# Low parts of 68 weight tiles of a decoder layer: written by ScalarE and an accumulating DMA in place of a subtraction on GpSimd

## The chip, the cores and the metric

The kernel runs on one core of a Trainium2 chip. The metric is the device time of one execution in microseconds (us). Below, PE is TensorE, DVE VectorE, ACT ScalarE, POOL GpSimd and SP SyncE, as the profile names them.

## The reference

One layer with three sub-layers, each ending in a LayerNorm over a residual sum. `u` is the modulated input of 512 rows and 1024 columns.

```python
# 1 and 3: SwiGLU feed-forward, 1024 -> 2 x 2816 -> 1024
# 2: token mixing
u = x * (1.0 + sc2) + sh2
q, k, v, glu_a, glu_b, gate_a, gate_b = jnp.split(u @ w_in[l], split_idx, axis=-1)   # 7 x 1024 columns
y_sb = stick_breaking_attention(heads(q), heads(k), heads(v))      # 16 heads of 64, strictly causal
y_sb = y_sb.transpose(0, 2, 1, 3).reshape(bsz, seq, SB_WIDTH) @ w_sb_out[l]
y_conv = conformer_conv(glu_a, glu_b, conv_w[l], conv_b[l], conv_ln_g[l], conv_ln_b[l]) @ w_conv_out[l]
merged = jax.nn.sigmoid(gate_a) * y_sb + jax.nn.sigmoid(gate_b) * y_conv
x = layer_norm(DEEPNORM_ALPHA * x + g2 * (merged @ w_out[l]), ln2_g[l], ln2_b[l])
```

`conformer_conv` is a causal convolution over 31 positions of each channel, then a LayerNorm and a swish. All data are float32.

## The kernel before

Every matrix product is made of three products in a shorter format (F32R): a value is split into a high part (a cast) and a low part (the value less its high part), and high x high, high x low and low x high are summed in PSUM. A weight tile of 128 x 1024 (512 KB) is loaded into one of three `raw` buffers, then `split_w` makes two tiles of it, `whi` by a cast on ACT (L113) and `wlo` by a subtraction, `raw - whi`, on POOL or DVE (L114). There are five buffers of each. `load_w` does this with POOL; `load_gated`, for weights that are scaled by a gate first (L127, on POOL), does it with DVE.

The second sub-layer, from about 405 to 1010 us, is written as a list of tasks. Each tile task has a part that fetches and splits a weight tile and one or two parts that multiply: `tile_tasks` for a block of 128 columns of q, k, the two halves of the GLU, or the gates ga and gb (24 PE instructions a tile), `v_tasks` for two tiles of w_v and four row blocks (psv, L594 to L596), `proj_tasks` for the output projections ysb and ycv. The first four tiles of w_in (q, k and the GLU halves of block 0) go through `dense_group` and are not touched by the change.

- Attention runs in 64 units (8 pairs of heads, 2 heads, 4 blocks of 128 rows). Unit i: three products give scores z; ACT makes two sigmoids of them (nb and be, L623, L624); DVE scans nb (L625); POOL masks be (L628) and multiplies it by nb (L630). Two units later PE transposes be into pw (L640), ACT casts it to wTh (L643), DVE makes the low part wTl (L644), and one unit after that PE multiplies with v into po (L663 to L665). Between the units stand the tile tasks, whose weights are fetched three tasks ahead.
- The convolution is made on DVE: for each of 8 channel blocks 31 taps (L511, L513 and 29 or so fused multiply-adds at L515) into cacc, and a sum (L520). They stand in a background list, from which 3.8 are taken for each attention unit and 14 after each ysb tile.
- When all taps are done, the convolution's rows are transposed on PE (pt, L766), normalised on DVE (cn, L776), transposed back (ptb, L787) and passed through a swish on ACT (L790). Then come the ycv projections. Meanwhile DVE also makes modulation vectors of the next sub-layer (ada, L179), whose rows are loaded into a ring of two buffers.

The order on each engine is set by a scheduler when the program is built; each engine then works through its own list in that order and waits for semaphores of the others. SP issues the loads (L101) in the same way.

Of the kernel before, what the change touches and what calls it, by code (L numbers as in the profile page):

```python
# [7 lines left out]
F32 = mybir.dt.float32  # L8
F32R = mybir.dt.float32r
BF16 = mybir.dt.bfloat16  # L10
AF = mybir.ActivationFunctionType
ALU = mybir.AluOpType
PSUM = bass.MemoryType.PSUM

P = 128
# [28 lines left out]
def decoder_block(ctx: ExitStack, tc: tile.TileContext, a: dict, out: bass.AP):  # L44
    nc = tc.nc

    core = ctx.enter_context(tc.tile_pool(name="core", bufs=1))
    wts = ctx.enter_context(tc.tile_pool(name="wts", bufs=1))
# [16 lines left out]
    def bank(name, tag="ps"):  # L65
        return banks["pool"].tile([P, 512], F32, tag=tag, name=name, bufs=banks["bufs"][tag])
# [33 lines left out]
    def load(dst, src, chain=False):  # L100
        ins = nc.sync.dma_start(dst, src).ins  # L101
        if "last" in issued:
            tc.add_manual_dep(ins, issued["last"].name,
                              mybir.DependencyInfo(mybir.DependencyClass.NoSync, mybir.DependencyReason.DATA),
                              reason="first loads in order of use")
        if chain:
            issued["last"] = ins


    def split_w(raw, lo_eng):  # L110
        hi = wts.tile([P, 1024], F32R, align_bytes=256, tag="whi", name="whi", bufs=5)
        lo = wts.tile([P, 1024], F32R, align_bytes=256, tag="wlo", name="wlo", bufs=5)
        nc.scalar.copy(hi, raw)  # L113
        lo_eng.tensor_sub(lo, raw, hi.bitcast(F32))  # L114
        return hi, lo

    def raw_tile(src, chain=False):
        raw = wts.tile([P, 1024], F32, tag="raw", name="raw", bufs=3)
        load(raw, src, chain)
        return raw  # L120

    def load_w(src, lo_eng=None):
        return split_w(raw_tile(src), lo_eng or nc.gpsimd)

    def load_gated(src, G):
        raw = raw_tile(src)
        nc.gpsimd.tensor_mul(raw, raw, G)  # L127
        return split_w(raw, nc.vector)

    def dense(ps, w, u, c0=0, c1=S, k0=0, k1=KC):  # L130
        (wh, wl), (uh, ul) = w, u
        for k in range(k0, k1):
            ks = slice(k * P, (k + 1) * P)
            nc.tensor.matmul(ps[:, c0:c1], wh[:, ks], mov(uh, k)[:, c0:c1], start=(k == 0), stop=False)  # L134
            nc.tensor.matmul(ps[:, c0:c1], wh[:, ks], mov(ul, k)[:, c0:c1], start=False, stop=False)  # L135
            nc.tensor.matmul(ps[:, c0:c1], wl[:, ks], mov(uh, k)[:, c0:c1], start=False, stop=(k == KC - 1))  # L136
# [229 lines left out]
    def dense_group(names, srcs, u, first, tags=None):  # L366
        ws = [load_w(s, nc.vector if first and i in FIRST_DVE else None) for i, s in enumerate(srcs)]
        pss = [bank(n, tag) for n, tag in zip(names, tags or ["ps"] * len(names))]
        if first:
            for c in range(2):  # L370
                for i, (ps, w) in enumerate(zip(pss, ws)):
                    dense(ps, w, u, c * 256, c * 256 + 256)
                    if c == 0 and i in LATE_AT and late:
                        late.pop(0)()
        else:
            for ps, w in zip(pss, ws):
                dense(ps, w, u)
        return pss
# [153 lines left out]
    def half_dense(st, name, ks, done):  # L532
        if ks == 0:
            st["ps"] = bank(name)
        dense(st["ps"], st["w"], u2, 0, S, ks * 4, ks * 4 + 4)
        if ks == 1:
            done(st["ps"])


    def tile_tasks(src, name, done):  # L540
        st = {}
        return [(lambda: st.update(w=load_w(src)), lambda: half_dense(st, name, 0, done)),
                (None, lambda: half_dense(st, name, 1, done))]

    def set_qk(j, x, ps):
# [2 lines left out]
    def qk_tasks(j):  # L548
        out_ = []
        for x, col in (("q", 0), ("k", 8)):  # L550
            out_ += tile_tasks(a["w_in"][col + j], x, lambda ps, x=x: set_qk(j, x, ps))
        return out_
# [11 lines left out]
    def glu_tasks(j):  # L564
        st = {}
        return (tile_tasks(a["w_in"][24 + j], "glua", lambda ps: st.update(a=ps))
                + tile_tasks(a["w_in"][32 + j], "glub", lambda ps: glu_done(j, st["a"], ps)))
# [10 lines left out]
    def v_tasks(q):  # L578
        st = {}

        def block(t):
            if t == 0:
                st["h"] = ap_.tile([P, NT, 256], F32R, tag="vh", name="vh", bufs=2)
                st["l"] = ap_.tile([P, NT, 256], F32R, tag="vl", name="vl", bufs=2)
                vq[q] = (st["h"], st["l"])
            if t % 2 == 0:
                st["ps"] = bank("psv")
            ps = st["ps"]
            o = ps[:, (t % 2) * 256 : (t % 2) * 256 + 256]
            tsl = slice(t * P, (t + 1) * P)  # L590
            for k in range(KC):
                wh, wl = st["w"][k // 4]
                cs = slice((k % 4) * 256, (k % 4) * 256 + 256)
                nc.tensor.matmul(o, u2[0][:, k, tsl], wh[:, cs], start=(k == 0), stop=False)  # L594
                nc.tensor.matmul(o, u2[0][:, k, tsl], wl[:, cs], start=False, stop=False)  # L595
                nc.tensor.matmul(o, u2[1][:, k, tsl], wh[:, cs], start=False, stop=(k == KC - 1))  # L596
            if t % 2 == 1:
                dst = st["h"][:, t - 1 : t + 1, :]
                pv = ps.rearrange("p (t e) -> p t e", t=2)
                nc.scalar.copy(dst, pv)  # L600
                nc.vector.tensor_sub(st["l"][:, t - 1 : t + 1, :], pv, dst.bitcast(F32))

        def fetch():
            st["w"] = [load_w(a["w_v"][q, h]) for h in range(2)]

        return [(fetch if t == 0 else None, lambda t=t: block(t)) for t in range(NT)]

# [101 lines left out]
    done = fetched = 0  # L709
# [93 lines left out]
    def proj_tasks(name, w, u, j, done):  # L803
        st = {}

        def half(ks):
            if ks == 0:
                st["ps"] = bank(name)
            dense(st["ps"], st["w"], u, 0, S, ks * 4, ks * 4 + 4)
            if ks == 1:  # L810
                done(j, st["ps"])

        return [(lambda: st.update(w=load_w(w[j])), lambda: half(0)), (None, lambda: half(1))]

    def sb(j):
        return proj_tasks("ysb", a["w_sb"], yp2, j, sb_done)
# [40 lines left out]
    for j in range(KC):  # L857
        if j + 2 < KC:
            run(gate_tasks("gb", j + 2))
        prefetch(2)  # L860
        run(proj_tasks("ycv", a["w_cv"], cp2, j, merge_done))
        bg(2)
# [115 lines left out]
```

## Time and profile before

| What | Value |
|---|---|
| Time, median of 3 runs | 1391.4 us (1390.05 to 1391.75) |
| The profiled execution | 1388.65 us, its span 1387.0 us |
| Busy, share of the span | PE 94%, DVE 59%, POOL 49%, ACT 33% |
| POOL's subtractions (L114) | 156, 398.7 us, 2560 ns each |
| ACT's casts of weights (L113) | 212, 220.8 us, 1046 ns each |
| DMA | 162.22 MB, mean 117 GB/s |

The span is the time from the first to the last instruction in the trace; the time of the execution has a little more around it. An engine's busy share is an average over the three sub-layers, which are limited by different things. In rows of waits, "PE po L664 <- DVE wTl L644: 19.4, 20, 4.6" reads: PE's instructions at L664 that write po waited for DVE's at L644 that write wTl, 19.4 us in total, 20 times, 4.6 us at the longest.

### The profile page before, as it was taken

How to read it: one execution, taken by the hardware profiler on the slowest of the kernel's cores; microseconds unless marked ns; L12 is line 12 of the kernel's file. 1: busy time of each engine (PE TensorE's matmuls, PEld its weight loads, DVE VectorE, ACT ScalarE, POOL GpSimd, SP SyncE). 2: the span in 40 equal slices, each digit the busy share in tenths (PEclk: the TensorE clock that was granted, in tenths of full speed). 3: DMA queues.
4: the chain of work that ended last, by engine and by line, in shares of the span. 5: the costliest groups of instructions: out<-in, count | busy, mean ns of one | idle time of the engine just before them, and what ended most of it. 6: DMA issues, size and time to landing. Idle time of an engine off the chain costs nothing.

```text
span 1387.0 us, 16644 instructions
## 1 busy us (share of the span) xinstructions
PE 1303.7 (94%) x6444; PEld 1076.4 (78%) x6444; DVE 817.2 (59%) x1017; ACT 458.0 (33%) x725; POOL 683.2 (49%) x392
## 2 busy tenths in 40 slices
PE   6899999999999998989998994998999999999997
PEld 4688888888897777767776873786898888888886
DVE  7876910454546968699899998516485100014545
ACT  2332322222254343434442422522263222222230
POOL 3474544644136675845555542355145366555433
PEclk9999999999999999999999997999999999999999
DMA  9669832323122221321122425323155233332221
GB/s 356 209 225 324 284 109 92 106 91 107 61 92 77 61 77 31 91 61 47 62 61 61 137 106 170 120 90 107 61 200 165 91 98 115 106 106 92 92 76 61
DMA packets 48063, 162.22 MB, mean 117 GB/s; under 512 B 5600, under 2 KB 5744, under 8 KB 47984
## 3 DMA queue, kind: packets, MB, share of 16 engines
q1 hardware_dynamic: 47952, 161.15, 35.6%
q8 instruction: 50, 0.82, 0.2%
q14 instruction: 29, 0.24, 0.1%
q0 software_dynamic: 32, 0.01, 0.0%
HBM read 159.04 MB, written 2.10 MB: 116 GB/s over the span
## 4 chain that ended last, share of the span: by engine, by line
PE 69%; DVE 25%; DMA 2%; issue 2%; POOL 1%; ACT 1%; SPq 0%; DVEq 0%; POOLq 0%; ACTq 0%
PE y L345 19%; DVE cacc L515 13%; DVE ada L179 3%; DVE nb L625 2%; DVE wTl L644 1%; PE psv L594 1%; PE gb L136 1%; PE gb L135 1%; PE ycv L135 1%; PE ycv L136 1%; PE gb L134 1%; PE ycv L134 1%; PE psv L596 1%; PE psv L595 1%; DMA ada<-in_ada_t 1%
## 5 line engine op out<-in xcount | busy, mean ns | idle before, releaser
L114 POOL TENSOR_TENSOR wlo<-raw,whi 128x1024 fp32r<-128x1024 f32 x156 | 398.7, 2560 | 363.2 <-ACT whi L113 351.3
L113 ACT CAST whi<-raw 128x1024 fp32r<-128x1024 f32 x212 | 220.8, 1046 | 407.5 <-issue 75.3
L515 DVE SCALAR_TENSOR_TENSOR cacc<-h,cv_w,cacc 128x512 f32<-128x512 f32 x232 | 237.0, 1080 | 0.0
L127 POOL TENSOR_TENSOR raw<-raw,mod_g 128x1024 f32<-128x1024 f32 x52 | 130.3, 2511 | 140.2 <-DMA raw<-in_dn 71.5
L114 DVE TENSOR_TENSOR wlo<-raw,whi 128x1024 fp32r<-128x1024 f32 x56 | 111.5, 1991 | 24.8 <-ACT whi L113 24.8
L345 PE MATMUL y<-whi,sh 128*128 128x512 f32 x352 | 113.8, 390 | 0.0
L345 PE MATMUL y<-wlo,sh 128*128 128x512 f32 x352 | 113.6, 389 | 0.0
L345 PE MATMUL y<-whi,sl 128*128 128x512 f32 x352 | 113.5, 389 | 0.0
L630 POOL TENSOR_TENSOR be<-be,nb 128x127 f32<-128x127 f32 (+1 forms) x64 | 53.4, 834 | 105.2 <-DVE nb L625 94.0
L179 DVE SCALAR_TENSOR_TENSOR ada<-ada,crow 128x512 f32<-128x512 f32 x96 | 91.8, 996 | 18.7 <-DMA ada<-in_ada_t 13.0
L410 DVE TENSOR_TENSOR sl<-sF,sh 128x512 fp32r<-128x512 f32 x44 | 45.3, 1031 | 85.1 <-ACT sh L409 85.1
L345 PEld LDWEIGHTS y<-wlo,sh 128*128 128x128 f32 x352 | 66.1, 188 | 13.7
L345 PEld LDWEIGHTS y<-whi,sl 128*128 128x128 f32 x352 | 66.1, 188 | 13.7
L345 PEld LDWEIGHTS y<-whi,sh 128*128 128x128 f32 x352 | 66.1, 188 | 13.6
L409 ACT CAST sh<-sF 128x512 fp32r<-128x512 f32 x44 | 27.1, 623 | 143.8 <-PE y L345 132.0
L625 DVE TENSOR_TENSOR_SCAN nb<-nb,future 128x127 f32<-128x127 f32 (+1 forms) x64 | 63.4, 990 | 1.4 <-ACT nb L623 1.4
L643 ACT CAST wTh<-pw 128x128 fp32r<-128x128 f32 (+1 forms) x64 | 27.2, 425 | 79.7 <-PE pw L640 79.6
L664 PE MATMUL po<-wTl,vh 128*64 128x128 f32 x160 | 32.9, 231 | 19.4 <-DVE wTl L644 19.4
L212 DVE SCALAR_TENSOR_TENSOR acc<-ada,silu_c,acc 128x1024 f32<-128x1024 f32 x21 | 43.7, 2080 | 12.3 <-DMA ada<-in_ada_w 11.9
L628 POOL TENSOR_SCALAR_AFFINE_SELECT be<-be 128x128 f32<-128x128 f32 x64 | 41.1, 642 | 8.9 <-ACT be L624 8.9
L452 PE MATMUL first<-uh,whi 128*128 128x512 f32 x64 | 27.2, 426 | 18.7 <-DVE uh L448 11.5
L664 PEld LDWEIGHTS po<-wTl,vh 128*64 128x64 f32 x160 | 21.7, 136 | 28.7 <-DVE wTl L644 25.3
(490 smaller groups left out, 3297.4 us busy)
## 6 DMA issues: line engine op xcount, KB each, us to landing
raw<-in_gu SPq DMA_DIRECT2D x80, 512.0 KB, 3.6
raw<-in_w_in SPq DMA_DIRECT2D x48, 512.0 KB, 3.6
raw<-in_dn SPq DMA_DIRECT2D x44, 512.0 KB, 3.5
ada<-in_ada_t SPq DMA_DIRECT2D x32, 512.0 KB, 4.5
ada<-in_ada_w SPq DMA_DIRECT2D x24, 512.0 KB, 4.7
ada<-in_ada SPq DMA_DIRECT2D x32, 256.0 KB, 6.0
raw<-in_gu_first SPq DMA_DIRECT2D x8, 512.0 KB, 6.5
raw<-in_w_v SPq DMA_DIRECT2D x8, 512.0 KB, 3.4
```

The costliest lines, as they stand in the source:

```text
L113: nc.scalar.copy(hi, raw)
L114: lo_eng.tensor_sub(lo, raw, hi.bitcast(F32))
L127: nc.gpsimd.tensor_mul(raw, raw, G)
L179: nc.vector.scalar_tensor_tensor(raw[:, qs], raw[:, qs], 1.0, crow[:, qs], ALU.mult, ALU.mult, accum_out=parts[:, q : q + 1])
L212: nc.vector.scalar_tensor_tensor(acc, raw, sc[:, k : k + 1], acc, ALU.mult, ALU.add)
L345: nc.tensor.matmul(acc[t][h][:, c0 - h * 512 : c1 - h * 512], st[:, tsl], wt[:, c0:c1], start=(k == 0 and i == 0 and c0 % 512 == 0), stop= ...
L410: nc.vector.tensor_sub(sl, sF[f], sh.bitcast(F32))
L515: ins = nc.vector.scalar_tensor_tensor(o, hv, cv_w[:, j, i : i + 1], o, ALU.mult, ALU.add)
L625: nc.vector.tensor_tensor_scan(nb[:, 1:n][:, ::-1], nb[:, 1:n][:, ::-1], future[:, S - n + 1 : S][:, ::-1], 1.0, ALU.mult, ALU.max)
L628: nc.gpsimd.affine_select(be[:, n - P : n], be[:, n - P : n], [[-1, P]], ALU.is_gt, 0.0, base=0, channel_multiplier=1)
L630: nc.gpsimd.tensor_mul(be[:, 0 : n - 1], be[:, 0 : n - 1], nb[:, 1:n])
L664: nc.tensor.matmul(po[0:DH, tsl], vh[:, sb, vs], wl[:, ss], start=False, stop=False)
```

## The change

A new function, `load_added`, takes the place of `load_w` in `tile_tasks`, `v_tasks` and `proj_tasks`: 44 tiles of w_in, 8 of w_v, 8 of w_sb and 8 of w_cv, 68 in all. ACT writes the cast `whi` as before, then the negative of it into `wlo`; POOL issues a DMA that reads the weight tile from HBM once more and adds it to `wlo` in place. The subtractions for the feed-forward sub-layers, the first four tiles of w_in and the gated weights stay.

```diff
+    def load_added(src):
+        raw = raw_tile(src)
+        hi = wts.tile([P, 1024], F32R, align_bytes=256, tag="whi", name="whi", bufs=5)
+        lo = wts.tile([P, 1024], F32R, align_bytes=256, tag="wlo", name="wlo", bufs=5)
+        nc.scalar.copy(hi, raw)
+        nc.scalar.mul(lo, hi.bitcast(F32), -1.0)
+        nc.gpsimd.dma_start(out=lo, in_=src, accum_op=ALU.add)
+        return hi, lo
...
-        return [(lambda: st.update(w=load_w(src)), lambda: half_dense(st, name, 0, done)),
+        return [(lambda: st.update(w=load_added(src)), lambda: half_dense(st, name, 0, done)),
...
-            st["w"] = [load_w(a["w_v"][q, h]) for h in range(2)]
+            st["w"] = [load_added(a["w_v"][q, h]) for h in range(2)]
...
-        return [(lambda: st.update(w=load_w(w[j])), lambda: half(0)), (None, lambda: half(1))]
+        return [(lambda: st.update(w=load_added(w[j])), lambda: half(0)), (None, lambda: half(1))]
```

In the changed program the cast is L130, the negative L131 and the DMA L132, and later lines stand ten further down. The lists of PE and DVE hold the same instructions in the same order as before. On POOL, early in attention, where the mask (AFFINE_SELECT) and the product of be stand between the weights' low parts, the list before is:

```order
L628 AFFINE_SELECT be_3255<-be_3255 128x128
L630 TENSOR_TENSOR be_3255<-be_3255,nb_3254 128x383
L114 TENSOR_TENSOR wlo_3560<-raw_3557,whi_3559 128x1024
L628 AFFINE_SELECT be_3292<-be_3292 128x128
L628 AFFINE_SELECT be_3336<-be_3336 128x128
L630 TENSOR_TENSOR be_3292<-be_3292,nb_3291 128x511
L304 TENSOR_TENSOR n0_2596<-n0_2596,raw_3327 128x1024
L114 TENSOR_TENSOR wlo_3673<-raw_3670,whi_3672 128x1024
```

and of the change, at the same place:

```order
L638 AFFINE_SELECT be_3260<-be_3260 128x128
L640 TENSOR_TENSOR be_3260<-be_3260,nb_3259 128x383
L638 AFFINE_SELECT be_3297<-be_3297 128x128
L132 DMA wlo_3567<-in_w_in 128x1024
L638 AFFINE_SELECT be_3341<-be_3341 128x128
L640 TENSOR_TENSOR be_3297<-be_3297,nb_3296 128x511
L314 TENSOR_TENSOR n0_2596<-n0_2596,raw_3332 128x1024
L640 TENSOR_TENSOR be_3341<-be_3341,nb_3340 128x127
L132 DMA wlo_3681<-in_w_in 128x1024
```

Each subtraction has become an issue of a DMA at about the same place in the list, one or two steps later.

On ACT, in the same units, where the casts of weights stand between attention's casts (wTh) and sigmoids (nb, be), the list before is:

```order
L113 CAST whi_3559<-raw_3557 128x1024
L525 CAST qh_3273<-q_3233 128x512
L643 CAST wTh_3279<-pw_3277 128x128
L623 ACTIVATE nb_3291<-z_3287 128x512
L624 ACTIVATE be_3292<-z_3287 128x512
L643 CAST wTh_3319<-pw_3316 128x256
L623 ACTIVATE nb_3335<-z_3331 128x128
L624 ACTIVATE be_3336<-z_3331 128x128
L113 CAST whi_3672<-raw_3670 128x1024
L525 CAST kh_3366<-k_3298 128x512
L643 CAST wTh_3380<-pw_3376 128x384
```

and of the change:

```order
L130 CAST whi_3566<-raw_3564 128x1024
L535 CAST qh_3278<-q_3238 128x512
L653 CAST wTh_3284<-pw_3282 128x128
L633 ACTIVATE nb_3296<-z_3292 128x512
L634 ACTIVATE be_3297<-z_3292 128x512
L131 ACTIVATE wlo_3567<-whi_3566 128x1024
L653 CAST wTh_3324<-pw_3321 128x256
L633 ACTIVATE nb_3340<-z_3336 128x128
L634 ACTIVATE be_3341<-z_3336 128x128
L130 CAST whi_3680<-raw_3678 128x1024
L535 CAST kh_3373<-k_3303 128x512
L131 ACTIVATE wlo_3681<-whi_3680 128x1024
```

The negative (L131) stands a few steps behind its cast, ahead of a later unit's wTh; nothing else changes places.

## The prediction, made before the changed kernel had run

> **What bounds the kernel now.** I read the page's chain first, then the busy time of the second sub-layer by stages, then what TensorE (PE) waits for there. The page's span and its chain, by engine and by line:
>
> ```profile
> span 1387.0 us, 16644 instructions
> PE 69%; DVE 25%; DMA 2%; issue 2%; POOL 1%; ACT 1%; SPq 0%; DVEq 0%; POOLq 0%; ACTq 0%
> ```
>
> PE carries the end, but a quarter of the chain lies on VectorE (DVE). The stages of the second sub-layer, one row each: attention with the convolution taps, the first output projections, the convolution's normalisation, the second projections. Columns: window, its length, busy us of PE, weight loads, DVE, ACT and POOL, granted clock, DMA share, GB/s.
>
> ```profile
> 428.00:757.00 329.00, 303.81 (x1799) 242.27 (x1798) 287.99 (x344) 131.00 (x271) 205.82 (x180) 0.98 0.20 62
> 757.00:828.00 71.00, 71.00 (x324) 58.82 (x323) 68.65 (x82) 23.45 (x30) 30.41 (x12) 1.00 0.35 117
> 828.00:876.00 48.00, 24.67 (x123) 19.75 (x122) 42.26 (x86) 16.68 (x37) 13.57 (x9) 0.79 0.50 167
> 876.00:962.00 86.00, 85.63 (x378) 70.59 (x376) 30.11 (x40) 26.43 (x36) 41.02 (x17) 1.00 0.34 104
> ```
>
> PE is idle 25.2 us in the first row (329.00 - 303.81) and 23.3 us in the third; in the second and fourth it is full. DVE is 88% busy in the first (287.99 of 329), 97% in the second and 88% in the third. PE's waits from 428 to 880 us (sum, times, longest):
>
> ```profile
> PE po L664 <- DVE wTl L644: 19.4, 20, 4.6
> PE ptb L787 <- DVE cn L776: 13.6, 3, 11.4
> PE pt L766 <- DVE cacc L520: 9.7, 1, 9.7
> PE k L134 <- DVE ql L526: 4.0, 2, 3.6
> PE psv L594 <- DVE vl L601: 1.6, 1, 1.6
> ```
>
> All five end on DVE: 48.3 us, as much as the two idle sums (48.5). POOL, whose work is removed, ends none of them. So the question is whether POOL's subtraction costs DVE anything. One subtraction on POOL, and the convolution tap that DVE runs at that moment, alone and with its two followers:
>
> ```profile
> 780.72 2.68 POOL L114 TENSOR_TENSOR wlo<-raw,whi 128x1024 fp32r<-128x1024 f32 x1 [2.78 <-ACT whi L113]
> 781.06 2.88 DVE L515 SCALAR_TENSOR_TENSOR cacc<-h,cv_w,cacc 128x512 f32<-128x512 f32 x1
> 781.06 4.21 DVE L515 SCALAR_TENSOR_TENSOR cacc<-h,cv_w,cacc 128x512 f32<-128x512 f32 x3
> ```
>
> The tap that meets the subtraction takes 2.88 us and ends with it; two more taps add 1.33 us, 0.665 us each. DVE stands still while POOL subtracts. All taps (nanoseconds min/median/max) and their busy time in the two stretches; the subtractions of both, and those in the first alone (nothing on DVE, 92.91 us on POOL):
>
> ```profile
> L515 DVE SCALAR_TENSOR_TENSOR cacc<-h,cv_w,cacc x232: 721/743/2907, 431.8 to 837.1; 128x512 f32<-128x512 f32 x116
> 428.00:757.00 329.00, 172.60 (x173) 0.98 0.20 62
> 757.00:876.00 119.00, 64.42 (x60) 0.91 0.41 137
> L114 POOL TENSOR_TENSOR wlo<-raw,whi x52: 2338/2479/4408, 426.3 to 872.9; 128x1024 fp32r<-128x1024 f32 x52
> 428.00:757.00 329.00, 0.00 (x0) 92.91 (x37) 0.98 0.20 62
> ```
>
> At 0.665 us each, 173 taps would take 115.0 us and 60 would take 39.9: the taps lose 57.6 and 24.5 us, 82.1 in all, to waiting for POOL.
>
> **The change, part by part.** It takes 68 subtractions off POOL (44 tiles of w_in, 8 of w_v, 8 of w_sb and 8 of w_cv; 52 of them in the row above) and adds, for each, an ACT pass over 128x1024, an issue on POOL and an accumulating DMA of 512 KB. TensorE's and DVE's orders stay as they are. The nearest rows of the additions: ACT's cast and its multiplication of a tile of that shape, the only DMA that POOL issues now (time on POOL, then time to landing), and the plain load of the same weights.
>
> ```profile
> L113 ACT CAST whi<-raw 128x1024 fp32r<-128x1024 f32 x212 | 220.8, 1046 | 407.5 <-issue 75.3
> L298 ACT ACTIVATE raw<-raw x4: 1059/1060/1061, 416.6 to 1153.5; 128x1024 f32<-128x1024 f32 x4
> L420 POOL DMA_DIRECT2D vec<-in_vecs x1: 735/735/735, 1.9 to 1.9; - x1
> vec<-in_vecs POOLq DMA_DIRECT2D x1, 8.0 KB, 5.7
> raw<-in_w_in SPq DMA_DIRECT2D x48, 512.0 KB, 3.6
> ```
>
> *POOL* goes from 52 x 2.48 = 129 us to 52 x 0.735 = 38 us in that stretch, and its attention steps (be) queue behind 0.7 instead of 2.5 us.
>
> *When the weights are ready.* Now a low part takes 2.48 us behind ACT's cast; afterwards 1.06 (ACT) + 0.74 (issue) + the landing. No row shows an accumulating DMA: the landing lies between 3.6 us (a load of that size) and 5.7 + 3.6 = 9.3 us (POOL's small DMA, plus a second pass over the bytes). I take 6: 7.8 us instead of 2.5. What hides it is the ring of five buffers:
>
> ```profile
> ACT whi L113 <- PE gb L135: 22.0, 5, 4.4
> L134 PE MATMUL gb<-uh,whi x64: 389/389/478, 874.3 to 944.5; 128*128 128x512 f32 x64
> L136 PE MATMUL ycv<-ph,wlo x64: 388/389/389, 891.2 to 961.2; 128*128 128x512 f32 x64
> ```
>
> ACT's cast waits for PE to leave the fifth-last tile, and 16 tiles (8 gb, 8 ycv) take 874.3 to 961.2 us, 5.43 each: a lead of four tiles, 21.7 us, even where PE is full. So the later arrival costs nothing there at 7.8 us, nor at the upper end's 11.1; without that cover it would be 5 to 9 us per tile. One place has less cover, the second weight tile of the first v block:
>
> ```profile
> 406.35 1.05 ACT L113 CAST whi<-raw 128x1024 fp32r<-128x1024 f32 x1 [6.43 <-PE q L135]
> L595 PE MATMUL psv<-wlo,uh x32: 283/283/283, 415.0 to 426.1; 128*128 128x256 f32 x32
> ```
>
> Its cast ends at 407.4; qh's cast (a fraction of a us) stands between it and the new pass, so the low part lands near 416 us; block t=0 needs it about 1.4 us after 415.0 (the four blocks take 11.1 us, 2.8 each, and the second tile serves the second half). That costs 0 to 3 us once; I take 1.
>
> Beside these rows the Trainium skill has a rule that speaks against the change: "Collectives: The Full Stack", section "The bandwidth ceiling: the fold count and why AG ≠ RS ≠ AR", says that an add in the DMA path reads two sources for each chunk written and so runs at half of a copy's rate. By it the landing would be an estimated 2 x 3.6 = 7.2 us, the weights 9.0 us behind the cast, and the sum below unchanged; no run here shows it yet.
>
> *SP.* The raw tile is free once ACT has cast it, no longer when POOL has subtracted, so loads go out about 2.5 us earlier; SP's order shifts at one place only (a load of crow and two of ada). Nothing waits for that: 0. *DMA.* 68 x 0.524 = 36 MB more are read in the sub-layer; the DMAs' share is 0.20 to 0.50 of the engines in the rows above. Bounds 0 to 3 us, for the ada rows below; I take 0.
>
> *ACT* gets 68 x 1.06 = 72 us more: in the attention stage 37 passes, 39 us on 131 of 329 us, 52% busy. Were none covered, attention's casts and sigmoids, which stand behind them, would cost PE those 39 us; but PE waits for ACT for next to nothing now (all five waits above end on DVE). Between 0 and 39 it is near 0: I take 2.
>
> *The gain in attention.* Of the 25.0 us that PE waits for wTl, ql and vl (19.4 + 4.0 + 1.6), how much goes? DVE's load falls from 288.0 to 230.4 us, 70%, and what stands ahead of wTl is a tap of 0.74, not 2.9 us. About 23 waits can remain at a quarter of a us (a tap or a scan in flight): 6 us. I take 19; bounds 0 and 25.
>
> *The gain at the convolution's normalisation.* The chain there, in order of time (start, length, what):
>
> ```profile
> 824.97 12.89 DVE cacc L515 x13
> 838.46 0.60 DVE cacc L520
> 839.70 3.79 DMA ada<-in_ada_t
> 844.93 5.14 DMA ada<-in_ada_t
> 851.50 3.72 DMA ada<-in_ada_t
> 855.95 0.73 DVE cn L776
> ```
>
> The last taps end at 838.5 us; the second stretch's excess of 24.5 us goes, and DVE comes here about 20 us earlier (it still waits for PE's ysb). PE's wait of 9.7 us for the last tap is gone whole. Then DVE runs modulation rows (ada) ahead of cn, each waiting for a load that goes out only when DVE has freed one of two buffers: three waits, which stay what they are but start up to 20 us earlier, against 9.7 us for PE. So about 10 of the 13.6 us go; what is late next is this ada ring, with 4 us. Bounds: 9.7 and 23.3; I take 19.3.
>
> *Clock.* The granted clock is 0.98 and 0.79 in the rows with PE's idle time and 1.00 in the full ones. 0.21 x 48 = 10 us is the most that can come back, and the idle time itself is most of it: I take 3.
>
> Sum: 19 + 19.3 + 3 - 2 - 1 = 38.3 us. The profiled execution took 1388.65 us (span 1387.0); that gives 1350.4. The median of the runs shown, 1391.4, lies 2.75 above it: 1391.4 - 38.3 = 1353, which is the prediction.
>
> **The rivals.**
>
> *Slower: the accumulating DMAs don't keep up.* The place is where PE takes a tile every 5.43 us: 26 tiles from 770 to 823 and 876 to 962 us. (53 us make 10 of them, beside the 16 above.) It decides once such a DMA holds the engines for longer than that: the excess times 26, less the lead of 21.7, against 38.3 gained, so from about 5.43 + 60/26 = 7.7 us each. At 10 us: 26 x 4.6 - 22 = 97 lost, 59 slower, 1450. Against it: a load lands in 3.6 us, latency included. For it: an addition in the DMA path appears in no row. 0.12.
>
> *Attention waits for ACT instead.* If half of the 39 us of passes reach PE through wTh, 20 us stand in place of the 2 taken: 38.3 - 18 = 20 gained, 1371. For it: ACT's queue is in order, and the new pass stands ahead of wTh at many places. Against: it would be half busy only. 0.17.
>
> *DVE stays shut out.* If POOL's issue of an accumulating DMA keeps DVE standing as long as the subtraction did (2.5 us, not 0.735), or DVE's taps keep POOL from issuing and attention's be waits behind it, the change doesn't do what matters: 1391, within 3 us. Against it: the one issue took 0.735 us, though with DVE idle. 0.07.
> The Trainium skill's "SBUF — State Buffer", section "SBUF: two separate sides", warns that POOL cannot write descriptors while a two-port DVE operation runs. Of DVE's work here only the short one-input operations could be such, not the taps; no trace here shows an issue under a busy DVE.
>
> *More than forecast.* All of the 48.3 us and 8 of clock: 1335. 0.04.
>
> **How the numbers follow.** The forecast, 1340 to 1366, has 0.60. Faster is the forecast, the ACT rival and the last: 0.60 + 0.17 + 0.04 = 0.81. Differences under 0.2% (2.8 us) can't be told from none here: 0.07. Slower: 0.12. For 8 in 10 the range takes in the forecast, the ACT rival and most of the last: from 1335 to 1384 (a gain of 7, where ACT takes back nearly all).
>
> **What would show it.** Taps at a maximum near 1.5 us instead of 2.9 (attention's own POOL steps remain), and DVE near 230 us in the attention stage; waits for wTl below 8 us; no wait of pt for cacc; ptb's wait for cn near 4 us, behind ada loads. An issue on POOL near 0.74 us and a landing of 4 to 9 us; no wait of PE for wlo but at the first v block. The forecast is wrong if PE's matmuls with wlo wait for DMAs, if wTh's waits for ACT grow by tens of us, or if taps still show 2.5 us.

## The result, and the profile after

| | before | after |
|---|---|---|
| Median of the runs taken beside each other | 1390.72 us (1388.86 to 1391.75) | 1339.18 us (1338.22 to 1342.05) |
| Span of the profiled execution | 1387.0 us | 1337.3 us |

The ratio is 0.9634, with an interval of 0.9616 to 0.9653: 51.5 us faster by the medians, 49.7 by the spans, where 38.3 had been forecast. The page of after, its span and its chain by engine:

```profile
span 1337.3 us, 16794 instructions
PE 82%; DVE 12%; DMA 3%; ACT 1%; POOL 1%; issue 1%; SPq 0%; DVEq 0%; POOLq 0%; ACTq 0%
```

DVE's share of the chain has halved, from 25% to 12%. What PE waits for from the start of the second sub-layer to the second projections (385 to 905 us):

```profile
PE ptb L797 <- DVE cn L786: 8.9, 2, 7.3
PE po L674 <- DVE wTl L654: 1.8, 3, 1.4
PE k L144 <- DVE ql L536: 0.8, 2, 0.4
PE psv L604 <- DVE vl L611: 0.5, 1, 0.5
PE q L144 <- DVE vl L611: 0.3, 1, 0.3
```

Before, the same view held 19.4 us for wTl, 13.6 for cn, 9.7 for cacc, 4.0 for ql and 1.6 for vl. The wait for cacc is gone, attention's are nearly gone, and of cn's two thirds are left. No wait of PE for wlo and none for ACT's casts stands in it.

To say where 49.7 us came from, the stages have to be cut at the same work, not at the same time: the windows below are set so that PE executes the same number of matmuls in each pair (x319 and x316, x1838 and x1839, x405 and x403). First the end of the first sub-layer with the first tiles of the second, then attention, then the ysb projections with the normalisation. Columns as in the prediction: window, length, busy us of PE, weight loads, DVE, ACT and POOL, granted clock, DMA share, GB/s. Before:

```profile
385.00:428.00 43.00, 40.85 (x319) 40.03 (x318) 15.43 (x18) 22.52 (x37) 17.07 (x9) 0.96 0.30 99
428.00:764.00 336.00, 310.81 (x1838) 248.12 (x1837) 294.95 (x354) 133.16 (x275) 206.97 (x181) 0.98 0.21 62
764.00:876.00 112.00, 88.67 (x405) 72.73 (x404) 103.94 (x157) 37.97 (x64) 42.83 (x19) 0.91 0.42 141
```

And after:

```profile
385.00:424.00 39.00, 38.89 (x316) 38.15 (x316) 12.55 (x18) 26.96 (x43) 8.12 (x9) 1.00 0.71 179
424.00:730.00 306.00, 302.56 (x1839) 244.42 (x1838) 247.45 (x356) 167.28 (x311) 146.05 (x180) 1.00 0.60 131
730.00:826.00 96.00, 86.98 (x403) 71.84 (x402) 75.82 (x155) 52.51 (x78) 16.07 (x19) 0.95 0.91 242
```

A stage's gain splits in two: idle time of PE (length less busy), and busy time for the same matmuls.

| Stage | gain | idle time of PE | busy time of PE |
|---|---|---|---|
| start | 4.0 | 2.2 to 0.1: 2.0 | 2.0 |
| attention | 30.0 | 25.2 to 3.4: 21.8 | 8.2 |
| projections and normalisation | 16.0 | 23.3 to 9.0: 14.3 | 1.7 |
| sum | 50.0 | 38.1 | 11.9 |

So about 38 us are waits that went and 12 us are busy time. Of these 12, 7 are stretches in which the clock was halved; most of the rest is, by an estimate, an overlap of matmuls that each wait breaks (both are worked out under the prediction's term for the clock). DVE's busy time in the attention stage falls from 295 to 247 us for the same work (x354 and x356). The rows of the change itself, first the groups of taps and of the new pass (busy us, mean ns of one):

```profile
L525 DVE SCALAR_TENSOR_TENSOR cacc<-h,cv_w,cacc 128x512 f32<-128x512 f32 x232 | 173.8, 807 | 0.0
L131 ACT ACTIVATE wlo<-whi 128x1024 fp32r<-128x1024 f32 x68 | 72.1, 1060 | 0.9
```

Then the line of the new issue (ns, minimum, median and maximum), with the landing of all 68, from the issue to the end of the transfer:

```profile
L132 POOL DMA_DIRECT2D wlo<-in_w_in x44: 856/875/892, 408.2 to 871.0; - x44
DMA to landing us min/median/max: 5.4/6.9/9.7
```

A tap takes 807 ns on average where it took 1080 (237.0 us in all). What still stretches taps is POOL's other work with two inputs. From the order of time early in attention (start, length), POOL's instructions first:

```profile
439.60 1.10 POOL L640 TENSOR_TENSOR be<-be,nb 128x511 f32<-128x511 f32 x1
440.66 2.83 POOL L314 TENSOR_TENSOR n<-n,raw 128x1024 f32<-128x1024 f32 x1
446.37 0.89 POOL L132 DMA_DIRECT2D wlo<-in_w_in  x1
```

And DVE's in the same stretch:

```profile
439.69 5.67 DVE L525 SCALAR_TENSOR_TENSOR cacc<-h,cv_w,cacc 128x512 f32<-128x512 f32 x4
446.66 1.46 DVE L525 SCALAR_TENSOR_TENSOR cacc<-h,cv_w,cacc 128x512 f32<-128x512 f32 x2
```

Four taps beside the two products take 5.67 us (the longest of all taps, 2.87, is among them); two taps take 1.46, 0.73 each, the first of them beside the new issue. The issue doesn't stop DVE, and the taps don't stop the issue: the 23 issues that ran beside taps took 865 to 887 ns.

### The profile page after: what moved, and what is told of

Read it like the earlier page. It is cut to its first block, busy times and chain, and to the rows that moved or that the text cites. A ratio compares the mean times of both kernels' runs of the same rounds, so it can differ in the third digit from the quotient of the medians.

```text
span 1337.3 us, 16794 instructions
## 1 busy us (share of the span) xinstructions
PE 1292.0 (97%) x6444; PEld 1069.7 (80%) x6444; DVE 737.6 (55%) x1017; ACT 523.0 (39%) x793; POOL 570.9 (43%) x392
## 3 DMA queue, kind: packets, MB, share of 16 engines
q1 hardware_dynamic: 47952, 161.15, 36.3%
q0 software_dynamic: 9824, 35.66, 15.8%
## 4 chain that ended last, share of the span: by engine, by line
PE 82%; DVE 12%; DMA 3%; ACT 1%; POOL 1%; issue 1%; SPq 0%; DVEq 0%; POOLq 0%; ACTq 0%
PE y L355 19%; DVE cacc L525 4%; DVE ada L189 3%; DMA ada<-in_ada_t 1%; PE z L628 1%; PE q L144 1%; PE glub L144 1%; PE glua L144 1%; PE pw L650 1%; PE ycv L146 1%; PE gb L146 1%; PE gb L144 1%; PE ycv L144 1%; PE gb L145 1%; PE ycv L145 1%; PE q L145 1%
## 5 line engine op out<-in xcount | busy, mean ns | idle before, releaser
L114 POOL TENSOR_TENSOR wlo<-raw,whi 128x1024 fp32r<-128x1024 f32 x88 | 224.5, 2556 | 250.9 <-ACT whi L113 237.3
L525 DVE SCALAR_TENSOR_TENSOR cacc<-h,cv_w,cacc 128x512 f32<-128x512 f32 x232 | 173.8, 807 | 0.0
L114 DVE TENSOR_TENSOR wlo<-raw,whi 128x1024 fp32r<-128x1024 f32 x56 | 106.5, 1902 | 26.7 <-ACT whi L113 26.7
L130 ACT CAST whi<-raw 128x1024 fp32r<-128x1024 f32 x68 | 71.4, 1049 | 126.7 <-PE ga L145 19.7
L355 PEld LDWEIGHTS y<-whi,sh 128*128 128x128 f32 x352 | 66.1, 188 | 13.6
L355 PEld LDWEIGHTS y<-wlo,sh 128*128 128x128 f32 x352 | 66.1, 188 | 13.6
L132 POOL DMA_DIRECT2D wlo<-in_w_in x44 | 38.4, 874 | 82.1 <-ACT wlo L131 78.3
L131 ACT ACTIVATE wlo<-whi 128x1024 fp32r<-128x1024 f32 x68 | 72.1, 1060 | 0.9
L635 DVE TENSOR_TENSOR_SCAN nb<-nb,future 128x127 f32<-128x127 f32 (+1 forms) x64 | 60.2, 941 | 2.0 <-ACT nb L633 1.8
L638 POOL TENSOR_SCALAR_AFFINE_SELECT be<-be 128x128 f32<-128x128 f32 x64 | 44.2, 691 | 22.9 <-ACT be L634 22.3
L222 DVE SCALAR_TENSOR_TENSOR acc<-ada,silu_c,acc 128x1024 f32<-128x1024 f32 x21 | 42.6, 2029 | 12.9 <-DMA ada<-in_ada_w 12.7
L654 DVE TENSOR_TENSOR wTl<-pw,wTh 128x128 fp32r<-128x128 f32 (+1 forms) x64 | 30.5, 477 | 32.5 <-ACT wTh L653 32.4
```

What stands on the lines that cost most here:

```text
L131: nc.scalar.mul(lo, hi.bitcast(F32), -1.0)
L355: nc.tensor.matmul(acc[t][h][:, c0 - h * 512 : c1 - h * 512], st[:, tsl], wt[:, c0:c1], start=(k == 0 and i == 0 and c0 % 512 == 0), stop= ...
L525: ins = nc.vector.scalar_tensor_tensor(o, hv, cv_w[:, j, i : i + 1], o, ALU.mult, ALU.add)
L635: nc.vector.tensor_tensor_scan(nb[:, 1:n][:, ::-1], nb[:, 1:n][:, ::-1], future[:, S - n + 1 : S][:, ::-1], 1.0, ALU.mult, ALU.max)
```

## The experiments

Four theories were to be told apart. A, the prediction's: DVE stands still while POOL's subtraction reads its two inputs, and that is what the change takes away. B: it is POOL's queue, in which attention's steps stood behind 2.5 us of subtraction. C: the loads start earlier, because a raw tile is free as soon as ACT has cast it. D: what is left is set by the accumulating DMAs, which share the engines with the ada loads. Ratios are to runs of the kernel before on the same chip; times are medians. Waits in the text are PE's from 385 to 905 us.

### The subtraction put back beside the change

```diff
+        junk = wts.tile([P, 448], F32, tag="junk", name="junk", bufs=1)
+        for c in (0, 448):
+            nc.gpsimd.tensor_sub(junk, raw[:, c : c + 448], hi[:, c : c + 448].bitcast(F32))
         nc.gpsimd.dma_start(out=lo, in_=src, accum_op=ALU.add)
```

> The changed kernel, and at each of the 68 places POOL also subtracts whi from raw into a scratch tile, in two pieces of 448 columns (about 1.1 us each), ahead of its DMA. The same occupation of POOL as in the run that only writes, but with two SBUF inputs. Theory A: most of the gain goes, 1370 to 1395 us, and taps that meet a piece take 1.2 to 2.9 us. Rival B: the same time as the run that only writes, within 5 us. Rival C (the gain comes from raw buffers that are free earlier, so that loads go out earlier): this run holds raw as long as before, so 1380 to 1391 us, but with taps as short as in the changed kernel.

It took 1394.86 us, ratio 1.0049 (1.0033 to 1.0065): the whole gain is gone and some 6 us more. PE's waits are the old ones:

```profile
PE ptb L800 <- DVE cn L789: 17.5, 3, 15.2
PE po L677 <- DVE wTl L657: 17.0, 17, 3.5
PE pt L779 <- DVE cacc L533: 8.0, 1, 8.0
```

The subtraction on POOL is the cause, whatever else the change brings. But it takes POOL's time, keeps the raw tile and shuts DVE out, all at once: this run alone doesn't tell A, B and C apart.

### POOL as long busy, without reading

```diff
+        for _ in range(5):
+            nc.gpsimd.memset(junk, 0.0)
         nc.gpsimd.dma_start(out=lo, in_=src, accum_op=ALU.add)
```

> The changed kernel, and at each of the 68 places POOL also writes zeros into a scratch tile five times (128x448, write only, no SBUF input), about 2.4 us, ahead of its DMA: POOL's queue is as occupied as with the subtraction, but reads nothing. Theory A (DVE stands still only while POOL's two-input operation reads SBUF; the gain is DVE's freed time): as the changed kernel, 1337 to 1346 us, taps no longer than about 1.6 us. Rival B (the gain is that attention's mask and product on POOL no longer queue behind 2.5 us of work): 1370 to 1391 us.

It took 1395.94 us, ratio 1.0039 (1.0027 to 1.0052), which looks like B and isn't. The memsets depend on nothing, and the scheduler moved all 340 of them to the front of the program, from 2.7 to 274.5 us:

```profile
L134 POOL MEMSET junk<- x340: 461/472/971, 2.7 to 274.5; 128x448 f32 x170
```

They held up the low parts of the first sub-layer, whose second products (y) began at 320.5 us in place of 264.5. The second sub-layer was as fast as after the change (cn 9.0 us, wTl 1.4). The run says nothing on the question. So the same memsets were held at their place in the program:

```diff
+        for _ in range(5):
+            tc.keep_in_program_order(nc.gpsimd.memset(junk, 0.0))
```

> The changed kernel with five memsets of 128x448 on POOL ahead of each accumulating DMA (340 in all, 0.47 us each, so 2.36 us per tile, about what the subtraction took), this time held at their place in the program's order. The memsets read nothing. Theory A (DVE stands still only while POOL's operation of two inputs reads SBUF): the taps keep a mean near 0.8 us and PE's waits for wTl stay under 5 us; the time stays with the changed kernel's, 1337 to 1348, the few us above it for issues that come 2.4 us later. Theory B (it is POOL's queue, in which attention's steps and the low parts stand behind 2.4 us of work): PE's waits come back, 1365 to 1391, with the taps at 0.8 us or not. Theory C (the loads start earlier because the raw tile is free after ACT's cast): loads are unchanged here, 1337 to 1345.

It took 1342.15 us, ratio 0.9655 (0.9631 to 0.9680). Its groups of taps and memsets:

```profile
L528 DVE SCALAR_TENSOR_TENSOR cacc<-h,cv_w,cacc 128x512 f32<-128x512 f32 x232 | 175.7, 815 | 0.0
L134 POOL MEMSET junk<- 128x448 f32 x340 | 173.1, 509 | 14.9
```

And its longest waits:

```profile
PE ptb L800 <- DVE cn L789: 11.2, 2, 9.5
PE po L677 <- DVE wTl L657: 2.1, 3, 1.4
```

173 us of POOL's time are occupied again, at the same places as before the change, and taps keep 815 ns. The span is 2.3 us longer, all of it at cn (11.2 us against 8.9). B is out: occupation of POOL's queue is worth about 2 us of the 50.

### POOL reading one input

```diff
+        for c in (0, 448):
+            nc.gpsimd.tensor_copy(junk, hi[:, c : c + 448].bitcast(F32))
         nc.gpsimd.dma_start(out=lo, in_=src, accum_op=ALU.add)
```

> The changed kernel with two copies of 128x448 on POOL per tile ahead of the accumulating DMA: one input from SBUF, where the subtraction has two. Theory A in its narrow form (it takes two inputs on POOL to keep DVE standing): taps keep a mean near 0.81 us, PE's waits stay small, 1337 to 1346, as with the memsets. Wide form (any reading by POOL does it): taps rise towards 1.0 us as with the subtraction, waits for wTl of 10 us or more come back, 1355 to 1395.

It took 1344.71 us, ratio 0.9669 (0.9655 to 0.9683). The waits stay small (wTl 3.1 us, cn 11.6). Taps and copies:

```profile
L528 DVE SCALAR_TENSOR_TENSOR cacc<-h,cv_w,cacc 128x512 f32<-128x512 f32 x232 | 184.5, 853 | 0.0
L134 POOL COPY junk<-whi 128x448 f32<-128x448 f32 x136 | 96.6, 711 | 105.6 <-ACT whi L130 101.8
```

A copy does stretch taps, by 184.5 - 173.8 = 10.7 us in all. By the starts and ends of both in the trace, taps and copies shared 34 us, so about a third of the shared time is lost to the taps. The subtraction in two pieces cost the taps 228.8 - 173.8 = 55 us over 83 us shared, two thirds; the memsets 1.9 over 64. What the taps don't lose, the copies mostly do: the 36 copies that began while a tap ran took 939 ns on average, the 11 that began ahead of a tap 558, and the 41 taps that began under a copy ended 0.55 us after it on average. So the one that starts second waits for the other. The narrow form of A holds for the time; that only two inputs do harm does not.

### The low parts on DVE

```diff
-        return [(lambda: st.update(w=load_w(src)), ...
+        return [(lambda: st.update(w=load_w(src, nc.vector)), ...
```

This is the kernel before, with the subtraction of all 68 tiles on DVE (the same edit in `v_tasks` and `proj_tasks`), no DMA and no negative.

> The kernel before, with the low parts of the same 68 tiles subtracted on DVE instead of POOL: no negative on ACT, no DMA. Theory A: DVE is no longer shut out (-57.6 us in the attention stage) but has 37 subtractions of 1.1 to 1.2 us there (+43 us), so about 274 of 329 us busy: a little faster than before, 1360 to 1388 us. Rival B: POOL's queue is as free as in the changed kernel, so about 1339 to 1350 us. Rival C: raw is held until DVE has come to it, at least as long as before: 1388 us or more.

It took 1354.54 us, ratio 0.9745 (0.9729 to 0.9760), better than A's numbers. The engines' busy time over its span, and then PE's waits:

```profile
PE 1302.4 (96%) x6444; PEld 1076.3 (80%) x6444; DVE 815.3 (60%) x1085; ACT 457.7 (34%) x725; POOL 516.1 (38%) x324
```

```profile
PE po L664 <- DVE wTl L644: 10.7, 8, 3.7
PE ptb L787 <- DVE cn L776: 4.5, 2, 2.8
PE k L134 <- DVE ql L526: 3.7, 2, 2.7
```

C is out as the main cause: a raw tile is held here until DVE has subtracted, not free after ACT's cast, and 35 us came all the same. DVE is busy for 815.3 us, where it was 817.2 before: over the whole span the subtractions cost it as much as standing still for POOL did. Yet the waits fall by more than half. The sum hides where DVE works. Attention and the stage behind it, cut at the same matmuls as in the rows before (x1838, and x403 for x405):

```profile
425.00:751.00 326.00, 310.93 (x1838) 249.74 (x1837) 282.26 (x385) 133.14 (x273) 122.13 (x143) 0.97 0.21 63
751.00:843.00 92.00, 87.37 (x403) 71.67 (x402) 85.04 (x146) 39.36 (x67) 3.20 (x4) 0.96 0.43 138
```

In attention DVE is busy for 282 us in place of 295, and the stage is 10 us shorter; at the normalisation it is 85 in place of 104, and 20 us shorter. Most of these 32 us of DVE's time stand again where PE doesn't wait for it: 25 us in place of 15 in the stretch ahead of attention, 204 in place of 189 behind the normalisation. So DVE's load in the stage, on which the prediction's working rests, goes with the gain here too. One more thing differs and wasn't tested by itself: the subtractions now stand at set places in DVE's list, while a stall meets whatever runs when POOL starts.

### The change without the accumulating DMA

```diff
-        nc.gpsimd.dma_start(out=lo, in_=src, accum_op=ALU.add)
```

The low part stays the negative of the high part, so the products with it leave out the weights' low bits.

> The changed kernel without the accumulating DMAs (the low part stays the negative high part). What it is faster by is what 68 issues on POOL and 36 MB of accumulating transfers still cost. Theory A (they are hidden by the ring of five buffers): 1334 to 1340 us. Rival D (their transfers hold up the loads of modulation rows that DVE waits for ahead of the convolution's normalisation, and of weights): 1326 to 1333 us, with PE's wait of ptb for cn of 8.9 us cut to under 4.

It took 1337.17 us, ratio 0.9620 (0.9598 to 0.9643). The spans of the profiled executions are 1337.5 without the DMAs and 1337.3 with them, but two of the four executions without them took 1334.9 us, at a mean clock of 0.997 and 0.996 against 0.992 in the profiled one. In the balance the DMAs cost between nothing and some 4 us. In the profiled execution that balance has two sides: cn's wait is 3.5 us here against 8.9, so the DMAs cost some 5 us at the normalisation; and attention, cut at x1837 matmuls, is 8 us longer here:

```profile
424.00:738.00 314.00, 308.06 (x1837) 249.37 (x1836) 246.22 (x356) 167.24 (x310) 112.32 (x143) 0.98 0.21 66
```

308.06 us busy against 302.56 is the clock (0.98), and 5.9 idle against 3.4. Why the clock dropped in this execution and not in that with the DMAs, the runs don't tell.

### One half each

First the change at the output projections' tiles alone, then at attention's tiles alone.

```diff
 # tile_tasks; the same in v_tasks
-        return [(lambda: st.update(w=load_added(src)), ...
+        return [(lambda: st.update(w=load_w(src)), ...
```

> The change at the 16 tiles of w_sb and w_cv and at the 8 of gb and the like that the projection tasks load, alone; the w_in tiles of attention and w_v keep POOL's subtraction. By theory A the gain is where the subtraction meets DVE's work: attention keeps its waits (po for wTl near 19 us, taps up to 2.9 us there), the normalisation's stretch gains what it gained, 10 to 16 us: 1373 to 1382. If the normalisation's gain is only DVE's backlog of taps from attention, it needs attention's part: 1382 to 1390.

The expectation counts 8 tiles of gb to this half; they go through `tile_tasks`, so the half is the 16 tiles of w_sb and w_cv. It took 1377.43 us, ratio 0.9909 (0.9883 to 0.9934): 12.8 us faster. wTl keeps 17.5 us, cn has 15.3, cacc none.

```diff
 # proj_tasks
-        return [(lambda: st.update(w=load_added(w[j])), lambda: half(0)), (None, lambda: half(1))]
+        return [(lambda: st.update(w=load_w(w[j])), lambda: half(0)), (None, lambda: half(1))]
```

> The other half: the change at the tiles that attention's tasks load (w_in by head, and w_v) alone; the projection tasks keep POOL's subtraction. By theory A: attention gains its 30 us, the wait of pt for cacc goes where it came from attention's backlog, the subtractions still stretch taps from 760 to 840 us: 1350 to 1362. Together with the run before, the two gains should add to about 50 us; if they add to over 60 or under 40, the two places share a wait.

It took 1352.02 us, ratio 0.9730 (0.9702 to 0.9759): 38.2 us faster, with 2.7 us left for wTl and 17.9 for cn. The halves add to 51.0 us, the whole is 51.5. By stages, cut at the same matmuls, attention's half gives all of attention's gain: 309 us in place of 336, where the other half leaves 336. At the normalisation both act: 112 us become 102 with the projections' tiles, 105 with attention's and 96 with both, and cacc's wait is gone with either half. Attention's half takes in tiles of ga and gb that are loaded in that very stretch, so whether it also leaves DVE a shorter backlog of taps is not told apart.

### The modulation rows behind the normalisation

What is left is cn's 8.9 us. The chain of after there (start, length, what):

```profile
784.34 5.82 DMA ada<-in_ada_t
791.59 5.72 DMA ada<-in_ada_t
798.75 6.74 DMA ada<-in_ada_t
806.21 0.73 DVE cn L786
```

These are the three waits that the prediction named, each longer than before (3.79, 5.14 and 3.72), in a stretch where the DMAs' share is 0.91. The next run holds DVE's 32 sums of these rows in program order, behind the normalisation (`pin` is passed as True for both sets of rows, sh3 and sc3).

```diff
-            nc.vector.scalar_tensor_tensor(raw[:, qs], raw[:, qs], 1.0, crow[:, qs], ALU.mult, ALU.mult,
-                                           accum_out=parts[:, q : q + 1])
+            ins = nc.vector.scalar_tensor_tensor(raw[:, qs], raw[:, qs], 1.0, crow[:, qs], ALU.mult, ALU.mult,
+                                                 accum_out=parts[:, q : q + 1])
+            if pin:
+                tc.keep_in_program_order(ins)
...
```

> The changed kernel with DVE's sums of the third set of modulation rows (ada, 32 sums) held in program order, which places them behind the convolution's normalisation instead of among it. Theory D (what is left of PE's wait for cn, 8.9 us, is set by the ring of two ada buffers whose loads now share the DMA engines with the accumulating DMAs): ptb's wait for cn falls under 3 us, the time to 1328 to 1336, unless the sums then arrive late for the projections that need them. Rival (the wait is the normalisation's own chain on DVE, and the ada loads only fill it): the wait stays at 7 to 9 us and the time at 1337 to 1342; if the pinned sums come too late, a wait of PE for them takes its place, 1340 to 1350.

It took 1332.78 us (1330.55 to 1336.51), ratio 0.9590 (0.9556 to 0.9624). The wait for cn is gone, and the stage is full at full clock:

```profile
730.00:814.00 84.00, 83.88 (x403) 70.04 (x402) 60.14 (x98) 51.03 (x75) 14.38 (x18) 1.00 0.87 195
```

96 us have become 84 for the same x403 matmuls. Where about half of that went again, PE's waits behind the second projections say:

```profile
PE y L357 <- DVE ml L888: 8.3, 1, 8.3
```

The sums now come late, and PE waits 8.3 us for ml, which had been 2.5. So the ring of ada rows set what was left, as D has it, and its 16 rows must still be loaded at some time; that the accumulating DMAs share in it stands on the run without them, where cn's wait was 3.5 us.

The last version holds the first two rows alone (`pin` is 2 for sh3 and 0 for sc3). It ran beside the change itself, timed once more.

```diff
-            column_sums(state["parts"][:, c, :], rows[c]["raw"], crow)
+            column_sums(state["parts"][:, c, :], rows[c]["raw"], crow, c < pin)
...
```

> The changed kernel with only the first two modulation rows' sums (four instructions on DVE) held in program order, behind the convolution's normalisation; the other rows can't come before them, since two buffers serve all rows, but may run as early as their loads allow afterwards. Theory D (the ada ring sets PE's last wait for cn): the wait for cn is gone as in the run that held all sums, and the sums end earlier than there (they ended at 912.7 us, and PE waited 8.3 us for ml behind them), so ml's wait is back near 3 us: 1326 to 1332. Rival (the order of sums among the merges makes DVE wait for ada loads ahead of the products that PE needs): ml's wait stays at 6 to 9 us or grows, 1331 to 1338.

> The changed kernel itself, timed again beside the two below: 1336 to 1342 by every theory.

The change took 1340.07 us, ratio 0.9634 (0.9621 to 0.9648); with the two rows held it took 1334.10, ratio 0.9600 (0.9578 to 0.9621). cn's wait is gone here too, but PE then waits 8.1 us for mh and 3.6 for ml behind the second projections. That is the rival's number: in the chain, the load of an ada row and its sums (883.1 to 892.5 us) still stand ahead of the merge. Both versions are about 6 us faster than the change by their medians, though the intervals of their ratios touch that of the change, and neither is told from the other.

## Why the prediction was right, and where its sizes were off

The mechanism was right: DVE was stopped by POOL's reading, PE waited for DVE, and the wait went with the subtraction. The time lies 0.8 us below the likeliest case's own range, 1340 to 1366. That it lies no further off is partly luck: the span gained 11.4 us more than the sum (49.7 against 38.3), although the normalisation was taken 4.9 too large. Term by term:

- *Attention, 19 taken, bounds 0 and 25.* The waits for wTl, ql and vl fell from 25.0 to 3.4 us: 21.6. The 6 us that were to remain, a quarter of a us at 23 places, were too many: 7 places are left.
- *Normalisation, 19.3 taken, bounds 9.7 and 23.3.* It was 14.4: 9.7 for cacc, as said, but 4.7 of cn's 13.6 and not 10. The failing step is "three waits, which stay what they are". They grew from 12.7 to 18.3 us in all, since the accumulating DMAs landed in the same stretch: there the ada rows land in 5.8 us (median, 730 to 826), and in 3.7 in the run without those DMAs. *DMA, 0 to 3, taken 0,* is the same mistake from the other side: 5 us here by the run without them.
- *Clock, 3 taken, 10 at most.* PE's busy time for the same matmuls fell by 9.9 us from attention on (8.2 + 1.7), and by 2.0 more ahead of it, where the step had looked at no window. The step took the one window with a low mean, 0.21 x 48 us, and reasoned that PE was idle there anyway. It overlooked the 0.98 of the attention row, in which stretches of 0.50 lie in the middle of full work. Before:

```profile
453.90:460.70 6.80, 6.77 (x32) 6.01 (x33) 6.80 (x8) 1.46 (x3) 4.18 (x4) 0.50 0.34 93
604.10:607.50 3.40, 3.40 (x9) 2.67 (x8) 3.27 (x5) 0.00 (x0) 0.27 (x1) 0.50 0.05 13
```

And after, at the first of these:

```profile
453.90:460.70 6.80, 6.80 (x61) 6.56 (x61) 6.80 (x9) 2.04 (x6) 4.31 (x4) 1.00 0.30 58
```

32 matmuls against 61 in the same 6.8 us. The two stretches hold 10.2 us of full work and lose half, 5.1 of attention's 8.2; a third, in the first v block's row below, loses 1.7 of the start's 2.0. At the normalisation 7.2 us of PE's work ran at 0.50 before and 6.0 after, which is 0.6 of its 1.7. So the clock gave 5.7 us from attention on, where 3 was taken, and 7.4 in all. What remains in attention, 3.1 us, is the waits themselves. Matmuls that follow each other overlap, and a wait breaks the overlap. Before:

```profile
518.66 0.22 PE L663 MATMUL po<-wTh,vh 128*64 128x128 f32 x1
519.33 0.27 PE L664 MATMUL po<-wTl,vh 128*64 128x128 f32 x1 [0.44 <-DVE wTl L644]
```

The second starts 0.67 us after the first. The next such pair, without a wait, starts 0.05 us apart (519.50 and 519.55). So this wait cost 0.62 us, of which 0.44 show as idle time and 0.18 stand in PE's busy time. With 23 waits down to 7, that makes about 2.9 us, an estimate from this one pair. The step priced a wait at its idle time alone.
- *The first v block, 1 us lost.* PE never waited for a low part. Instead the start gained 4.0 us, which no step had. PE waited 2.1 us for n (ps_tr at L275) there, and the clock was low behind it. DVE before, POOL before, DVE after, and the clock before:

```profile
392.25 2.84 DVE L264 TENSOR_SCALAR n<-r,mv,rstd 128x1024 f32<-128x1024 f32 x1 [0.73 <-POOL rstd L258]
```

```profile
392.18 2.36 POOL L114 TENSOR_TENSOR wlo<-raw,whi 128x1024 fp32r<-128x1024 f32 x1
```

```profile
391.99 0.81 DVE L274 TENSOR_SCALAR n<-r,mv,rstd 128x1024 f32<-128x1024 f32 x1 [0.73 <-POOL rstd L268]
```

```profile
395.80:399.20 3.40, 3.40 (x19) 3.40 (x17) 1.30 (x2) 3.36 (x9) 0.00 (x0) 0.51 0.40 145
```

The same instruction of DVE takes 2.84 us under the first subtraction for w_v and 0.81 without it.
- *ACT, 0 to 39, taken 2.* No wait of PE for wTh is left in the view of after, so 0. The pass took 1060 ns, as in its row.
- *Readiness of the weights.* The issue took 0.875 us, not 0.735; the landing 6.9 (5.4 to 9.7), where 6 was taken between 3.6 and 9.3. The lead of four tiles hid all of it.
- *The signs.* Waits for wTl under 8 us, none for cacc, none for wlo: as said. DVE near 230 us in the attention stage: no, 247 (295 before). Taps at a maximum near 1.5 us: no, 2.87, for the eight products n x raw on POOL (L314) were overlooked. The tap's floor was set too low with them: 0.665 is that of two taps in a row, while without the subtractions 232 taps kept DVE busy for 173.8 us, 0.749 each. So the taps lost 237.0 - 173.8 = 63 us to the subtractions, not 82.

The rival of a DMA that can't keep up had its deciding point at 7.7 us of the engines each. By the queues' shares of the page it is 15.8% of 1337.3 us over 68 transfers, 3.1 us. The landings by group, and the queues of the page:

```profile
raw<-in_w_in SPq DMA_DIRECT2D x48, 512.0 KB, 3.7
wlo<-in_w_in POOLq DMA_DIRECT2D x44, 512.0 KB, 7.1
```

```profile
q1 hardware_dynamic: 47952, 161.15, 36.3%
q0 software_dynamic: 9824, 35.66, 15.8%
```

7.1 us against 3.7 is close to twice, and so are 3.1 us of the engines against 1.6 for a plain load's bytes (36.3% of the span over 161.15 MB, for 0.524 MB). The Trainium skill's "Collectives: The Full Stack", section "The bandwidth ceiling: the fold count and why AG ≠ RS ≠ AR", has it that an add in the DMA path reads two sources and so runs at half of a copy's rate; these rows agree. What the Trainium skill's "SBUF — State Buffer", section "SBUF: two separate sides", warns of, descriptors held up under a two-port operation of DVE, shows at two issues at most. The longest of the 68, 1095 and 983 ns, are the two beside which DVE ran two one-input operations in a row (TENSOR_SCALAR into cacc, L521 and L523); the 44 of w_in took 856 to 892.

## What to carry to other kernels

Before counting an engine as idle cover, look at what its neighbour's instructions do at the same moment: a group with a median of 743 ns and a maximum of 2907 says that something stops it, and the overlap in time names it. Read an engine's load in the stage that waits for it: its sum over the span can stay the same (815 and 817 us) while the kernel gains 35 us. A wait of TensorE can cost more than its idle time: compare PE's busy time for the same number of matmuls. And when a change adds transfers, look for the ring of two buffers whose loads stand in the same stretch; here 8.9 of 23.3 us of waiting stayed there.

## What the runs showed of the hardware

- How much DVE loses to POOL goes with what POOL's instruction reads: of the time shared with taps about nothing for a memset, a third for a copy of one input, and two thirds for a subtraction of two (1.9 of 64, 10.7 of 34 and 55 of 83 us). Between taps and copies the one that started second waited: copies begun while a tap ran took 939 ns on average, those begun ahead of a tap 558. The Trainium skill's "SBUF — State Buffer", section "SBUF: two separate sides", speaks of an exclusive lock for the whole instruction, between a DVE operation of two inputs and a POOL operation that reads; the memsets and the copies agree.
- An accumulating DMA of 512 KB took 0.87 us on POOL, 6.9 us to land and 3.1 us of the engines' time, about double a plain load in the last two.
- The halved clock came in stretches of 3.4, 6.8 and 10.2 us before and after the change, also where PE was full: three of those, 13.6 us, stand between 395 and 608 us before (0.50 to 0.51), and the clock of the same windows is 1.00 after.
